# Eleven adding transfers of an attention kernel's MLP weights, issued in other rounds

## The chip, the cores and the metric

The kernel runs on one core of a Trainium2 chip. The metric is the time of one execution on the device in microseconds. Before the change it was 1013.88 us (median of 3 runs, 1013.76 to 1014.07).

The engines go by the names that the profile gives them: PE is TensorE (with PEld, its weight loads), DVE is VectorE, ACT is ScalarE, POOL is GpSimd, and SP issues transfers. Transfers run on 16 DMA engines that all queues share. Each engine runs its instructions in program order; semaphores hold an instruction back until what it reads is there.

## The reference

One layer of a diffusion backbone: a mixing sub-layer (pooling beside neighbourhood attention) and a squared-ReLU MLP, each inside an adaLN-modulated norm. 1024 latent tokens, 256 context tokens, width 1024, 8 heads of 64, all in fp32.

```python
h_x = _modulate(x, g_pre_mix[l], sh1, sc1)
h_c = _modulate(ctx, g_pre_mix[l], csh1, csc1)
u_x, q_x, k_x, v_x = _project(h_x, w_in[l])
u_c, q_c, k_c, v_c = _project(h_c, w_in[l])
attn_x = _neighbourhood_attention(q_x, k_x, v_x, k_c, v_c, rpb[l])
mix_x = jnp.concatenate([_pool_mixer(u_x, pool_w[l], pool_scale[l]), attn_x], axis=-1) @ w_out[l]
x = x + gt1 * _rmsnorm(mix_x, g_post_mix[l])
y_x = _sq_relu_mlp(_modulate(x, g_pre_mlp[l], sh2, sc2), w_mlp_in[l], w_mlp_out[l])
x = x + gt2 * _rmsnorm(y_x, g_post_mlp[l])

def _sq_relu_mlp(h, w1, w2):
    return jnp.square(jax.nn.relu(h @ w1)) @ w2
```

In the attention, each query sees an 8 x 16 window of the 16 x 64 grid with a position bias (`rpb`), and all 256 context keys, in one softmax.

## The kernel before, in words

Every product is split into a high and a low part (three matmuls for one, `three`), and the large products are made from seven block products with sums of blocks instead of eight. Two such sums of blocks of the MLP's second weight, `w2`, are this case's subject: t3q (8 groups) and t1d (8 groups), each group a 128 x 2 x 512 block of fp32, 512 KB, in DRAM. A group is made in two transfers. SP copies one block of `w2` there (`block_copied`, line 1327), and later GpSimd issues a transfer that reads another block of `w2` and adds it to what lies there (`block_summed`, which calls `add_to`, line 210). The list `block_sums` holds the sixteen adds in order, t3q's eight first; whoever calls `block_summed` takes the next. They are called sums below. The MLP reads t3q and t1d back hundreds of microseconds later.

Between the projections and the output projection lies the attention, 32 rounds (`for i in range(N)`), one for each pair of heads j and each block of 128 tokens m, in an order written out by hand. A round i issues, among others:

- `scores(i)`: TensorE, two heads' scores into two PSUM tiles;
- `biased(i, e)`: VectorE adds the bias table and takes the minimum; in the first of the two, `share(i - 1)` takes the reciprocals ri of unit i-1 and GpSimd spreads them over 64 columns into rb (line 1260). In the profile that is POOL L1260 COPY rb<-ri, rb9 for unit 9 and so on;
- in rounds 11, 19 and 27 two adding transfers of finished heads (`right_added`: y<-f and ss<-f), in rounds 15, 23 and 31 one more (f<-ss), all from GpSimd;
- `jobs`: a table of GpSimd's own work by round: the bias tables of the next heads (`built`, L1077), splits of operands into high and low parts (L1090, L1091: qP, kP, mix, wo), two small gathers (L816: sc2, s2);
- `block_copied`, then as many `block_summed` as the round's number stands in the table `SUMS`;
- `turn(i - 2)`: TensorE transposes, first rb of unit i-2, then its probabilities; a transpose's first step is a weight load (PEld L1276);
- `exps` (ScalarE), copies out of PSUM, and `values(i - 3)` (PE L1310).

GpSimd's instructions keep this order (`first_pool`, an ordering of that engine). So a sum stands on GpSimd behind the round's jobs and ahead of the next round's copy rb; and in GpSimd's DMA queue (q0) among the other adding transfers. The adding transfers of GpSimd take eight completion semaphores in turn.

After the rounds come the sums of the output projection. Loads of weights by SP (to_0w to to_3w, in `raw` and `page` buffers) are combined by adding transfers of GpSimd (to_0w<-in_w_out and to_1w<-in_w_out in round 31's wake, then y<-f, ss<-f, to_2w<-to_0w, to_3w<-to_1w). VectorE's products mp<-pox,Ga (line 1386, `out_kept`) write pages that to_0w and to_1w held, and so wait until the adds that read those have landed; TensorE's sums poz take the PSUM tile that these products read. Five more sums stand there, with rows 0 to 7 of the residual, and are not touched.

Of the kernel before, what the change touches and what calls it, by code (L numbers as in the profile page):

```python
# [103 lines left out]
def hybrid_block(ctx, tc, x, ctx_in, w_mod, mod_pages, w_u, b_mod, gp1, gp2, w_in, pool_w, rpb, w_out, w1, w2, vectors,  # L104
# [1081 lines left out]
    def block_summed():  # L1186
        to, of, g = block_sums.pop(0)
        add_to(to(g), of(g))
# [5 lines left out]
    with (  # L1194
# [132 lines left out]
        def block_copied():  # L1327
            to, i, g = block_copies.pop(0)
            nc.sync.dma_start(to(g), w2_block(i, 1, g))
# [2 lines left out]
        kks = (0, 1, 2, 3)  # L1332
        raw_o, wo = {}, {}
        LOADS = (16, 20, 26, 28)
        SUMS = (9, 11, 12, 14, 15, 16, 19, 22, 23, 27, 30)
        lows = []

        def high(src, hi, lo, pool=False):
# [73 lines left out]
        with in_order(ET.PE, ET.Activation, ET.DVE, ET.SP) as projected:  # L1412
# [34 lines left out]
            for i in range(N):  # L1447
# [26 lines left out]
                if block_copies and (i < 4 or 6 < i):  # L1474
                    block_copied()
                for _ in range(SUMS.count(i)):
                    block_summed()
# [1010 lines left out]
```

## Time and profile before

| | |
|---|---|
| median of 3 runs | 1013.88 us |
| the profiled execution | 1014.29 us, of which the span that the profile covers is 1012.5 us |
| PE busy | 1002.7 us, 99% of the span |
| DVE, ACT, POOL busy | 78%, 57%, 20% |
| granted TensorE clock | 0.999 |
| GpSimd's DMA queue (q0) | 18640 packets, 38.45 MB |
| SP's DMA queue (q1) | 111024 packets, 181.63 MB |
| attention's rounds | about 214 to 314 us |

Times in rows are microseconds from the start of the span. A row of the timeline has start, duration, engine, line, operation, output and inputs, and in brackets how long the engine stood idle before it and what ended that. A row of the waits has who waited for what, the total in us, how often, and the longest. A row of the DMA view has the median time from issue to landing.

### The profile page before, as it was taken

The numbers are of one execution on the slowest core, as the hardware profiler recorded it, in microseconds if no ns is written. First come the engines' busy times: TensorE is split into PE (matmuls) and PEld (weight loads), VectorE is DVE, ScalarE is ACT, GpSimd is POOL, SyncE is SP. The second block draws the span as 40 slices with busy tenths as digits, with TensorE's granted clock in tenths as the row PEclk, the third lists the DMA queues.
The fourth block names the chain that finished last, engine by engine and source line by source line (L and its number), as shares of the span: only waits on it lengthen the run. The fifth ranks groups of instructions, "written<-read, shape, count | busy, mean of one in ns | idle before, by whom it ended". The sixth has DMA issues, their size and how long they took to land.

```text
span 1012.5 us, 17059 instructions
## 1 busy us (share of the span) xinstructions
PE 1002.7 (99%) x6298; PEld 843.5 (83%) x6298; DVE 785.4 (78%) x1216; ACT 573.4 (57%) x988; POOL 203.7 (20%) x278
## 2 busy tenths in 40 slices
PE   8999999999999999999999999999999999999997
PEld 5788888878998888888888888888889888888886
DVE  5588767968885689879998888755797877877895
ACT  6672254448886746786555544555555455544451
POOL 4111200167985232410000000000001010021121
PEclk9999999999999999999999999999999999999999
DMA  9999799655989979986776667625999999579944
GB/s 365 392 295 323 248 260 310 210 154 198 229 183 247 233 196 273 298 210 202 262 250 219 204 201 235 210 75 188 357 354 302 289 339 310 161 212 315 305 180 163
DMA packets 146883, 252.13 MB, mean 249 GB/s; under 512 B 10416, under 2 KB 76848, under 8 KB 146800
## 3 DMA queue, kind: packets, MB, share of 16 engines
q1 hardware_dynamic: 111024, 181.63, 52.6%
q0 software_dynamic: 18640, 38.45, 19.7%
q10 hardware_dynamic: 17136, 30.97, 8.2%
q8 instruction: 49, 0.80, 0.3%
q14 instruction: 34, 0.28, 0.1%
HBM read 197.52 MB, written 69.22 MB: 263 GB/s over the span
## 4 chain that ended last, share of the span: by engine, by line
PE 97%; DVE 1%; ACT 1%; DMA 1%; POOL 0%; issue 0%; SPq 0%; DVEq 0%; POOLq 0%; ACTq 0%
PE pu L476 4%; PE pa L1310 3%; PE S L1223 3%; PE phx L221 3%; PE pyx L221 3%; PE phv L221 3%; PE phz L221 3%; PE pyx L222 3%; PE phx L222 3%; PE phx L223 3%; PE phv L223 3%; PE phz L223 3%; PE phz L222 3%; PE phv L222 3%; PE pyx L223 3%; PE pyz L221 1%
## 5 line engine op out<-in xcount | busy, mean ns | idle before, releaser
L1930 ACT ACTIVATE c<-c 128x512 f32<-128x512 f32 x48 | 30.3, 632 | 44.2 <-DVE c L2052 24.5
L1254 ACT ACTIVATE sp<-sp,nm 128x640 f32<-128x640 f32 (+1 forms) x64 | 51.4, 804 | 6.1 <-DVE ri L1258 4.8
L1243 DVE CUSTOM_DVE_ANT_0 sp<-S,tab 128x640 f32<-128x640 f32 (+1 forms) x56 | 44.5, 795 | 13.0 <-PE pz L1276 7.6
L169 ACT CAST wpS<-S 128x512 fp32r<-128x512 f32 x64 | 38.7, 616 | 28.0 <-PE phv L223 9.7
L221 PE MATMUL phx<-thB,wpA 128*128 128x512 f32 x128 | 50.2, 392 | 0.0
L222 PE MATMUL phx<-tlB,wpA 128*128 128x512 f32 x128 | 49.9, 389 | 0.0
L223 PE MATMUL phx<-thB,wpA 128*128 128x512 f32 x128 | 49.8, 389 | 0.0
L175 DVE TENSOR_TENSOR wpS<-S,wpS 128x512 fp32r<-128x512 f32 x64 | 43.4, 686 | 7.5 <-ACT wpS L169 7.4
L211 POOL DMA_DIRECT2D t<-in_w x16 | 19.3, 1208 | 105.5 <-DMA t<-t1d 61.9
L1931 ACT ACTIVATE c<-c 128x512 f32<-128x512 f32 x48 | 30.3, 630 | 15.1 <-DVE sa L2015 12.1
L238 POOL MEMSET accb<- 128x1024 f32 x1 | 1.0, 956 | 142.1 <-ACT c L1931 142.1
L221 PEld LDWEIGHTS phx<-thB,wpA 128*128 128x128 f32 x128 | 24.0, 188 | 5.5 <-ACT s L1983 0.4
L223 PEld LDWEIGHTS phx<-thB,wpA 128*128 128x128 f32 x128 | 24.0, 188 | 5.0
L222 PEld LDWEIGHTS phx<-tlB,wpA 128*128 128x128 f32 x128 | 24.0, 188 | 4.9
L1310 PE MATMUL pa<-pt,v 128*64 128x128 f32 x352 | 25.8, 279 | 0.0
L221 PE MATMUL phv<-thT,wpA 128*128 128x512 f32 x64 | 25.0, 391 | 0.0
L221 PE MATMUL phz<-thB,wpS 128*128 128x512 f32 x64 | 25.0, 391 | 0.0
L223 PE MATMUL phv<-thT,wpA 128*128 128x512 f32 x64 | 24.9, 389 | 0.0
L223 PE MATMUL phz<-thB,wpS 128*128 128x512 f32 x64 | 24.9, 389 | 0.0
L222 PE MATMUL phz<-tlB,wpS 128*128 128x512 f32 x64 | 24.9, 389 | 0.0
L221 PE MATMUL phy<-thT,wpS 128*128 128x512 f32 x64 | 24.9, 389 | 0.0
L222 PE MATMUL phy<-tlT,wpS 128*128 128x512 f32 x64 | 24.9, 389 | 0.0
(1200 smaller groups left out, 3683.0 us busy)
## 6 DMA issues: line engine op xcount, KB each, us to landing
hrA<-hdA SPq DMA_DIRECT2D x24, 512.0 KB, 7.5
wm<-in_mod_pages SPq DMA_DIRECT2D x16, 512.0 KB, 9.3
wa_0w<-in_w SPq DMA_DIRECT2D x16, 512.0 KB, 5.0
wa_1w<-in_w SPq DMA_DIRECT2D x16, 512.0 KB, 4.3
hdA<-c ACTq DMA_DIRECT2D x32, 256.0 KB, 2.2
hdS<-sa ACTq DMA_DIRECT2D x32, 256.0 KB, 2.6
hqS<-sb ACTq DMA_DIRECT2D x32, 256.0 KB, 4.1
b<-in_w SPq DMA_DIRECT2D x16, 512.0 KB, 8.6
```

What stands on the lines that cost most here:

```text
L169: nc.scalar.copy(hi, src)
L175: nc.vector.tensor_tensor(lo, src, hi.bitcast(F32), sub)
L221: nc.tensor.matmul(ps, ahi, bhi, start=first, stop=False, skip_group_check=more)
L222: nc.tensor.matmul(ps, ahi, blo, start=False, stop=False, skip_group_check=more)
L223: nc.tensor.matmul(ps, alo, bhi, start=False, stop=last, skip_group_check=more)
L476: nc.tensor.matmul(pus[b][j], wk(wgt, k, low, j * P, P), r, start=(k == 0 and n == 0), stop=(k == KT - 1 and n == 2))
L1223: nc.tensor.matmul(S[e][:, c0 : c0 + k[0].shape[1]], q[n_q][hs, cols], k[n_k][hs], start=(n_q + n_k == 0), stop=(n_q == 1))
L1243: nc.vector.tensor_tensor_reduce(out=to, in0=s, in1=bt, scale=1.0, scalar=BIG, op0=add, op1=ALU.min, accum_out=nm)
L1254: nc.scalar.activation(sp, sp, AF.Exp, bias=least[i, e], scale=-1.0, accum_out=sums[i][:, e : e + 1])
L1310: nc.tensor.matmul(pa[e * HD : (e + 1) * HD, cols], v[:, f : f + HD], turns[i][:, e, c] if c < 4 else fifths[i][:, :, (e + 1) * HD : (e + ...
L1930: nc.scalar.activation(r, src, AF.Relu)
L1931: nc.scalar.activation(r, r, AF.Square)
```

## The change

One table of round numbers is changed: the eleven sums of the rounds are issued in rounds 9, 10, 10, 12, 16, 18, 24, 25, 26, 29 and 30 in place of 9, 11, 12, 14, 15, 16, 19, 22, 23, 27 and 30. Their number, order and sizes stay.

```diff
@@ -1332,7 +1332,7 @@
         kks = (0, 1, 2, 3)
         raw_o, wo = {}, {}
         LOADS = (16, 20, 26, 28)
-        SUMS = (9, 11, 12, 14, 15, 16, 19, 22, 23, 27, 30)
+        SUMS = (9, 10, 10, 12, 16, 18, 24, 25, 26, 29, 30)
         lows = []
```

The order of instructions changes on GpSimd alone. GpSimd from round 10's copy (rb9) to round 12's (rb11), before and then changed; sc2 and tab00 are round 10's jobs, y0 and ss0 the adds of round 11, t3q0 a sum:

```order
L1260 COPY rb9_2867<-ri_9_2865 128x128
L816 DMA sc2_962<-gsc_2511 128x8x1
L1077 TENSOR_TENSOR tab00_2007<-msk_1900,U2_2803 128x128 x3
L1260 COPY rb10_2934<-ri_10_2932 128x128
L211 DMA y0_1345<-f0_2407 128x512
L211 DMA ss0_2107<-f0_2407 128x512
L211 DMA t3q0_2092<-in_w2 128x2x512
L1260 COPY rb11_3005<-ri_11_3003 128x128
```

```order
L1260 COPY rb9_2867<-ri_9_2865 128x128
L816 DMA sc2_962<-gsc_2511 128x8x1
L1077 TENSOR_TENSOR tab00_2007<-msk_1900,U2_2803 128x128 x3
L211 DMA t3q0_2092<-in_w2 128x2x512 x2
L1260 COPY rb10_2936<-ri_10_2934 128x128
L211 DMA y0_1345<-f0_2407 128x512
L211 DMA ss0_2107<-f0_2407 128x512
L1260 COPY rb11_3006<-ri_11_3004 128x128
```

Two sums now stand ahead of rb10, and ahead of y0 and ss0; the one behind ss0 is gone.

GpSimd in rounds 14 to 16, before and then changed; qP3 and mix0_5 are splits, f0<-ss0 is the add of round 15, which reads what ss0<-f0 of round 11 wrote:

```order
L1090 CAST qP3_0_3159<-q0_2_1970 128x512
L1091 TENSOR_TENSOR qP3_0_3159<-q0_2_1970,qP3_0_3159 128x512
L211 DMA t3q0_2092<-in_w2 128x2x512
L1260 COPY rb14_3227<-ri_14_3225 128x128
L211 DMA f0_2407<-ss0_2107 128x512
L211 DMA t3q1_2093<-in_w2 128x2x512
L1260 COPY rb15_3299<-ri_15_3297 128x128
L1090 CAST mix0_5_3304<-f1_2984 128x512
L1091 TENSOR_TENSOR mix0_5_3304<-f1_2984,mix0_5_3304 128x512
L211 DMA t3q1_2093<-in_w2 128x2x512
L1260 COPY rb16_3371<-ri_16_3369 128x128
```

```order
L1090 CAST qP3_0_3160<-q0_2_1970 128x512
L1091 TENSOR_TENSOR qP3_0_3160<-q0_2_1970,qP3_0_3160 128x512
L1260 COPY rb14_3227<-ri_14_3225 128x128
L211 DMA f0_2407<-ss0_2107 128x512
L1260 COPY rb15_3298<-ri_15_3296 128x128
L1090 CAST mix0_5_3303<-f1_2985 128x512
L1091 TENSOR_TENSOR mix0_5_3303<-f1_2985,mix0_5_3303 128x512
L211 DMA t3q1_2093<-in_w2 128x2x512
L1260 COPY rb16_3370<-ri_16_3368 128x128
```

The sums of rounds 14 and 15 are gone; round 16 keeps one.

GpSimd in rounds 24 to 26 and the start of 27, before and then changed; wo0_0 is a split of a weight, y2 the first add of round 27:

```order
L1260 COPY rb23_3868<-ri_23_3866 128x128
L1090 CAST mix0_6_3873<-f2_3558 128x512
L1091 TENSOR_TENSOR mix0_6_3873<-f2_3558,mix0_6_3873 128x512
L1260 COPY rb24_3939<-ri_24_3937 128x128
L1090 CAST qP3_1_3944<-q1_2_1902 128x512
L1091 TENSOR_TENSOR qP3_1_3944<-q1_2_1902,qP3_1_3944 128x512
L1260 COPY rb25_4008<-ri_25_4006 128x128
L1090 CAST wo0_0h_4013<-wor0_0_3277 128x512
L1091 TENSOR_TENSOR wo0_0l_4014<-wor0_0_3277,wo0_0h_4013 128x512
L1260 COPY rb26_4074<-ri_26_4072 128x128
L211 DMA y2_1441<-f2_3558 128x512
```

```order
L1091 TENSOR_TENSOR mix0_6_3870<-f2_3557,mix0_6_3870 128x512
L211 DMA t3q1_2093<-in_w2 128x2x512
L1260 COPY rb24_3937<-ri_24_3935 128x128
L1090 CAST qP3_1_3942<-q1_2_1902 128x512
L1091 TENSOR_TENSOR qP3_1_3942<-q1_2_1902,qP3_1_3942 128x512
L211 DMA t3q1_2093<-in_w2 128x2x512
L1260 COPY rb25_4007<-ri_25_4005 128x128
L1090 CAST wo0_0h_4012<-wor0_0_3276 128x512
L1091 TENSOR_TENSOR wo0_0l_4013<-wor0_0_3276,wo0_0h_4012 128x512
L211 DMA t1d_0_2084<-in_w2 128x2x512
L1260 COPY rb26_4074<-ri_26_4072 128x128
L211 DMA y2_1441<-f2_3557 128x512
```

Each of the three rounds now has a sum behind its split.

## The prediction

> **What bounds the kernel now.** I read the page's first and fourth parts first, then the stage of the change in stretches of three microseconds, then the waits inside it.
>
> ```profile
> PE 1002.7 (99%) x6298; PEld 843.5 (83%) x6298; DVE 785.4 (78%) x1216; ACT 573.4 (57%) x988; POOL 203.7 (20%) x278
> ...
> PE 97%; DVE 1%; ACT 1%; DMA 1%; POOL 0%; issue 0%; SPq 0%; DVEq 0%; POOLq 0%; ACTq 0%
> ```
>
> TensorE is busy for 99% of the span and makes 97% of the chain that ended last. So a transfer has no price of its own here: it costs what it makes TensorE wait, and there is next to nothing to win. GpSimd's 20% is an average over the program. In the attention stage, 214 to 322 us, it reads otherwise (columns: stretch, sum, then busy PE, PEld, DVE, ACT, POOL, the granted clock, the DMA share, GB/s):
>
> ```profile
> 254.00:257.00 3.00, 3.00 (x60) 2.76 (x56) 2.54 (x8) 2.79 (x8) 2.79 (x5) 1.00 1.01 156
> 296.00:299.00 3.00, 3.00 (x51) 2.73 (x51) 2.57 (x8) 2.56 (x8) 2.23 (x4) 1.00 1.12 223
> ```
>
> A round of attention is one such stretch, 2.8 to 3.0 us. GpSimd is nearly as full as TensorE, and the DMA engines are full too. TensorE depends on GpSimd once a round: rb(i), the copy at line 1260, is what turn(i) transposes first, and turn(i) runs in round i+2. The stage's waits name it:
>
> ```profile
> POOL rb L1260 <- DVE ri L1258: 11.8, 12, 2.3
> PEld pa L1276 <- POOL rb L1260: 0.3, 1, 0.3
> ```
>
> GpSimd often waits for its reciprocal, so it has time over in a dozen rounds; TensorE waited for the copy once by name. What counts is where the change uses up that time.
>
> **The change part by part.** Eleven sums leave rounds 9, 11, 12, 14, 15, 16, 19, 22, 23, 27, 30 and stand in 9, 10, 10, 12, 16, 18, 24, 25, 26, 29, 30. None is added, none grows. GpSimd's own rows (start, duration) around the first places:
>
> ```profile
> 248.77 1.22 POOL L211 DMA_DIRECT2D t3q<-in_w  x1 [0.19 <-issue]
> ...
> 252.71 1.28 POOL L1077 TENSOR_TENSOR tab<-msk,U 128x128 f32<-128x128 f32 x3
> 253.96 0.29 POOL L1260 COPY rb<-ri 128x128 f32<-128x128 f32 x1
> ...
> 255.08 1.18 POOL L211 DMA_DIRECT2D ss<-f  x1
> 255.64 1.81 POOL L211 DMA_DIRECT2D t3q<-in_w  x1
> ...
> 259.63 1.42 POOL L211 DMA_DIRECT2D t3q<-in_w  x1
> ...
> 264.64 1.29 POOL L1091 TENSOR_TENSOR qP<-q,qP 128x512 fp32r<-128x512 f32 x1
> 265.87 1.15 POOL L211 DMA_DIRECT2D t3q<-in_w  x1
> 266.61 0.70 POOL L1260 COPY rb<-ri 128x128 f32<-128x128 f32 x1
> 266.84 1.34 POOL L211 DMA_DIRECT2D f<-ss  x1
> 267.43 1.96 POOL L211 DMA_DIRECT2D t3q<-in_w  x1
> 268.47 1.22 POOL L1260 COPY rb<-ri 128x128 f32<-128x128 f32 x1
> ...
> 272.29 0.70 POOL L1260 COPY rb<-ri 128x128 f32<-128x128 f32 x1
> ...
> 314.08 1.28 POOL L211 DMA_DIRECT2D to_0w<-in_w_out  x1
> 315.41 1.22 POOL L211 DMA_DIRECT2D to_1w<-in_w_out  x1
> ```
>
> A sum is t3q<-in_w here, a copy rb<-ri. In round 14 the subtraction that starts at 264.64 ends at 265.93, and rb14 ends at 267.31: 1.38 us for a sum and a copy, and a copy alone is 0.29 (253.96), so a sum costs GpSimd 1.1 us. Two back to back have no row; nearest are the two large adds after the last round, 1.33 us apart (314.08 and 315.41). So two cost 2.2 to 2.66, and I take 2.4.
>
> *Round 10, two sums ahead of rb10.* The tables end where rb10 starts now, 253.96; with 2.4 and the copy's 0.29 it ends at 256.65. TensorE takes its copies by weight loads:
>
> ```profile
> 255.48 0.14 PEld L1276 LDWEIGHTS pa<-ident,rb 64*128 64x128 f32 x1
> 267.36 0.13 PEld L1276 LDWEIGHTS pa<-ident,rb 64*128 64x128 f32 x1
> 270.33 0.14 PEld L1276 LDWEIGHTS pa<-ident,rb 64*128 64x128 f32 x1
> ```
>
> The first is rb10's, at 255.48: late by 1.2 (1.0 to 1.45). Queued behind it on TensorE are the rest of turn(10), values(9) and the scores of round 13, so the whole stage moves. **+1.2.** The second is rb14's: the copy ended at 267.31 and the load came 0.05 later, so TensorE stood there; the only wait with that name is 0.3, and I take 0.2 (0 to 0.3). Round 14 loses its sum: **-0.2**. Rounds 11 and 12 carry the lateness on, y, ss and the s2 transfer standing in front as before, but TensorE has moved by 1.2 too and rb11 to rb13 just fit.
>
> *Round 15, the add f<-ss.* It reads ss, written by the add of round 11, and GpSimd stands still at it until that add has landed. The times from issue to landing, in the order of issue (sum of round 9, ss, sum of round 11, sum of round 12), and GpSimd's queue over 245 to 292 us:
>
> ```profile
> t3q<-in_w POOLq DMA_DIRECT2D x1, 512.0 KB, 11.6
> ss<-f POOLq DMA_DIRECT2D x1, 256.0 KB, 9.9
> t3q<-in_w POOLq DMA_DIRECT2D x1, 512.0 KB, 11.9
> t3q<-in_w POOLq DMA_DIRECT2D x1, 512.0 KB, 12.1
> ...
> q0 software_dynamic: 2780, 5.18, 63.9%
> ```
>
> With the starts above they land at 260.4, 265.0, 267.5 and 271.7: as they were issued. y stands between the first two and is as large as ss. 63.9% of 47 us is 30 us of all engines for 5.18 MB, 3.0 us for a 512 KB sum. Now ss is 1.8 us ahead of its reader. After the change two sums stand in front of y and ss that stood behind. The same five transfers then end with ss, at the latest when the five end now, 271.7; at the earliest at 260.4 + 2 x 3.0 + 2 x 1.5 = 269.4. I take 271.0, since the late end is measured with the same traffic on the other queue. The add then starts at 271.0; f and the copy take 1.28 (rb14's end to rb15's, 267.31 to 269.69, is 2.38 with a sum in it). rb15 ends at 272.28, for a load that would stand at 270.33 + 1.2 - 0.2 = 271.33. **+0.9** (0 to 1.6). Behind the waiting add stand rb15, the split of round 16 and its sum: that round takes 3.3 (rb15's end to rb16's, 269.69 to 272.99) where TensorE's takes 2.9. **+0.4** if the first is late.
>
> *Rounds 24, 25, 26: a sum each.* Their copies wait for the reciprocal now, and rb26 has its load at 302.30:
>
> ```profile
> 295.11 0.29 POOL L1260 COPY rb<-ri 128x128 f32<-128x128 f32 x1 [0.77 <-DVE ri L1258]
> ...
> 297.98 0.29 POOL L1260 COPY rb<-ri 128x128 f32<-128x128 f32 x1 [0.64 <-DVE ri L1258]
> ...
> 300.75 0.29 POOL L1260 COPY rb<-ri 128x128 f32<-128x128 f32 x1 [0.54 <-DVE ri L1258]
> ...
> 302.30 0.13 PEld L1276 LDWEIGHTS pa<-ident,rb 64*128 64x128 f32 x1
> ```
>
> The waits sum to 1.95; three sums take 3.3. The 1.35 that is left meets 1.26 from rb26's end, 301.04, to its load. **+0.1** (0 to 0.4). Rounds 22, 23, 27 gain only idle time.
>
> *After the stage.* Five sums now run from round 24 on, where two and the tail of two others did. The chain they reach (two adds of GpSimd, a product of VectorE, a matmul of TensorE, and both queues over 300 to 345 us):
>
> ```profile
> 336.24 0.86 POOL L211 DMA_DIRECT2D to_2w<-to_0w  x1 [9.46 <-DMA to_2w<-in_w_out]
> 337.47 0.86 POOL L211 DMA_DIRECT2D to_3w<-to_1w  x1 [0.37 <-issue]
> ...
> 344.45 0.69 DVE L1386 TENSOR_TENSOR mp<-pox,Ga 128x512 f32<-128x512 f32 x1 [1.77 <-DMA to_3w<-to_1w]
> ...
> 345.99 0.39 PE L221 MATMUL poz<-to_0h,S 128*128 128x512 f32 x1
> ...
> q0 software_dynamic: 2236, 4.73, 60.1%
> q1 hardware_dynamic: 3122, 6.26, 40.9%
> ```
>
> The matmul needs the bank that the product started at 344.45 frees, at 345.14: 0.85 us of room. That product waits for an add, the add for a load, and the load shares engines that the two queues fill to 101%. One sum more in that stretch is 3.0 us of engine time. If the DMA engines had room for it nothing moves; if the backlog of the rounds before comes on top (half a sum more) it is 4.5. I take the middle, 2.25, less 0.85: **+1.4** (0 to 3.6).
>
> The sums' own readers are far off, the first of them the loads of t1d from 750.4 us on (count, durations in ns, first and last start):
>
> ```profile
> L2139 SPq DMA_DIRECT2D t<-t1d x8: 325/658/3363, 750.4 to 835.1; - x8
> ```
>
> The order of the other four engines is the same as before.
>
> Sum: 1.2 - 0.2 + 0.9 + 0.4 + 0.1 + 1.4 = 3.8 us. The profiled execution took 1014.29 with a span of 1012.5, so it would show 1016.3 and 1018.1; it lies 0.4 above the median of the runs, 1013.88, to which I add: **1017.7 us**.
>
> [...]
>
> **The rivals.** *The queue has room.* If a 256 KB add does not wait for the sums in front of it, ss lands before 269.9 and f does not wait; if the spare 0.85 us at poz is not used up either, only round 10's own stall stays: 1.2 - 0.2 = +1.0, 1014.9, not to be told from before. It decides at those two points. For it: transfers on one queue run on sixteen engines side by side, and 101% is a mean that may hold gaps at the right place. Against it: the landings in order of issue, 60% of the engines in GpSimd's own queue. 25%.
>
> [...]
>
> *Nothing waits, and the old waits go.* rb could start 0.74 us after a sum's start (265.87, 266.61). If two sums cost only that, rb10 ends at 253.96 + 1.48 + 0.29 = 255.73, 0.25 late; round 14 gives back 0.2 to 0.3, and with no wait behind f or poz the time is 1013.9, at best 1013.6. For it: TensorE waits little anywhere. Against it: the copy after a sum lasted 0.70, not 0.29. 6%.
>
> *The backlog carries through.* All terms at their upper bounds: 1.45 - 0.2 + 1.6 + 0.4 + 0.4 + 3.6 = 7.25, 1021.1. For it: 101% on the engines. Against: several of them would have to be at the bound. 14%.
>
> **How the numbers follow.** Forecast 55%. Differences under 0.2%, 2.0 us, cannot be told from none here. Slower: forecast and backlog, 69%, and the edge of the queue rival 2%, 71%. Same: 26%. Faster by over 2 us: 3%, since the waits that the rows show gone sum to a few tenths. The range, 1014.2 to 1020.8, holds the forecast and the rival of the queue with room; it leaves out the rival without waits and the upper part of the backlog.
>
> **What would show it.** Right: the load of turn(10)'s copy waits about 1 us for GpSimd; f<-ss in round 15 waits for a DMA, 2 to 4 us; rb14 no longer holds TensorE; the to_3w add starts 1 to 3 us later relative to the last round and poz waits for the product. Wrong: a weight load of rb that never waits, or a stage of attention as long as before.

## The result, and the profile after

The changed kernel took 1024.69 us (median of 6 runs, 1019.28 to 1025.11), against 1013.88 us for the kernel before: a ratio of 1.0092, with a 95% interval of 1.0080 to 1.0103. It is slower, by 10.8 us where 3.8 were forecast. Two more sets of runs on other occasions gave 1021.46 and 1021.59 (ratios 1.0081 and 1.0074). The profiled execution shown here took 1022.3 us with a span of 1020.5.

The busy line, the clock by fortieths of the span and the chain, of the page of the changed kernel:

```profile
PE 1005.4 (99%) x6298; PEld 845.5 (83%) x6298; DVE 785.4 (77%) x1216; ACT 573.2 (56%) x988; POOL 203.4 (20%) x278
...
PEclk9999999999899999999999999999999999999999
...
PE 93%; DMA 2%; POOL 2%; issue 1%; ACT 1%; DVE 1%; SPq 0%; DVEq 0%; POOLq 0%; ACTq 0%
```

GpSimd's busy time is the same, 203.4 against 203.7. TensorE's grew by 2.7 us with the same 6298 matmuls, and one fortieth of the clock reads 8: some matmuls ran slower. The rest of the 8 us is idle time of TensorE. The waits of the attention stage say where:

```profile
POOL f L211 <- DMA ss<-f: 7.2, 1, 7.2
PEld pa L1276 <- POOL rb L1260: 5.6, 3, 4.2
...
PE pa L1276 <- POOL rb L1260: 4.9, 2, 4.0
```

GpSimd waits once for a transfer, for 7.2 us, where it did not wait before. TensorE's weight loads wait 5.6 us for GpSimd's copies, against 0.3 us before, and its matmuls wait 4.9 us in two places where none waited before. GpSimd's rows, in order of time, around the first two sums that stand together and around the wait:

```profile
253.91 2.37 POOL L211 DMA_DIRECT2D t3q<-in_w  x2
255.35 1.23 POOL L1260 COPY rb<-ri 128x128 f32<-128x128 f32 x1
255.59 1.87 POOL L211 DMA_DIRECT2D y<-f  x1
256.18 2.16 POOL L211 DMA_DIRECT2D ss<-f  x1
...
266.76 0.29 POOL L1260 COPY rb<-ri 128x128 f32<-128x128 f32 x1
274.26 0.91 POOL L211 DMA_DIRECT2D f<-ss  x1 [7.21 <-DMA ss<-f]
274.88 0.59 POOL L1260 COPY rb<-ri 128x128 f32<-128x128 f32 x1
```

And TensorE's first transposes of the two late copies, rb10 and rb15:

```profile
256.63 0.27 PE L1276 MATMUL pa<-ident,rb 64*128 64x64 f32 x1 [0.89 <-POOL rb L1260]
...
275.53 0.36 PE L1276 MATMUL pa<-ident,rb 64*128 64x64 f32 x1 [4.00 <-POOL rb L1260]
```

Stretches of two microseconds around the second (busy PE, PEld, DVE, ACT, POOL, then the granted clock, the DMA share, GB/s):

```profile
270.00:272.00 2.00, 1.53 (x22) 1.15 (x16) 1.29 (x5) 1.46 (x5) 0.00 (x0) 1.00 1.09 264
272.00:274.00 2.00, 0.00 (x0) 0.00 (x0) 1.21 (x5) 0.00 (x0) 0.00 (x0) 1.00 0.94 255
274.00:276.00 2.00, 0.47 (x8) 0.47 (x10) 0.00 (x0) 0.07 (x1) 1.74 (x3) 0.70 0.47 109
276.00:278.00 2.00, 2.00 (x27) 1.88 (x26) 0.69 (x1) 2.00 (x6) 1.91 (x3) 0.50 0.65 114
278.00:280.00 2.00, 2.00 (x18) 1.67 (x16) 0.29 (x1) 0.37 (x2) 1.92 (x4) 0.50 0.35 42
280.00:282.00 2.00, 2.00 (x32) 1.93 (x30) 0.98 (x4) 0.38 (x3) 0.71 (x1) 0.59 1.04 179
282.00:284.00 2.00, 2.00 (x36) 1.83 (x34) 1.46 (x5) 2.00 (x5) 1.86 (x3) 1.00 0.29 51
```

TensorE stands from 271.5 to 275.5. When it starts again the granted clock is 0.50, as it is from 274.8 to 281.6 (read in quarter microseconds). The twelve matmuls pa<-pt,v of that round take 1.55 us; such twelve take 0.88 in the kernel before, at a clock of 1.00.

The loss can be dated by the starts of the first rb transpose of each round: the distance from one to the next, less the same distance before the change. Three profiled executions of the changed kernel (the first above, two from the experiments), in us:

```
                                   first    second   third
round 10's late copy               +1.07    +1.05    +1.05
the wait for ss in round 15        +4.08    +2.42    +2.66
the round behind that wait         +2.38    +0.45    +1.50
other rounds                       +0.16    -0.09    -0.01
poz, after the stage               +0.28    +0.63    +2.08
near 398 us                        +0.24    +0.26    +0.18
sum                                +8.21    +4.72    +7.46
start of the stage                 -0.17    -0.28    -0.45
execution, against 1014.29 before  +8.0     +4.4     +7.0
```

The first line is steady. The wait, the round behind it and poz vary by 1.7 to 1.9 us each from execution to execution. The runs of the changed kernel spread over 6 us, while those of the kernel before lie within 0.5 us beside them and within 2.2 on every other occasion. No profiled execution is as slow as the median of the first six runs, 1024.69: the slowest shows 8.0 of the 10.8 us, and where the rest went is not shown.

### The profile page after: what moved, and what is told of

Same layout as the page of the kernel before. It is cut to its first block, busy times and chain, and to the rows that moved or that the text cites. A ratio compares the mean times of both kernels' runs of the same rounds, so it can differ in the third digit from the quotient of the medians.

```text
span 1020.5 us, 17064 instructions
## 1 busy us (share of the span) xinstructions
PE 1005.4 (99%) x6298; PEld 845.5 (83%) x6298; DVE 785.4 (77%) x1216; ACT 573.2 (56%) x988; POOL 203.4 (20%) x278
## 4 chain that ended last, share of the span: by engine, by line
PE 93%; DMA 2%; POOL 2%; issue 1%; ACT 1%; DVE 1%; SPq 0%; DVEq 0%; POOLq 0%; ACTq 0%
PE pu L476 4%; PE phx L221 3%; PE pyx L221 3%; PE phz L221 3%; PE phv L221 3%; PE pyx L222 3%; PE phx L222 3%; PE pyx L223 3%; PE phz L223 3%; PE phv L223 3%; PE phx L223 3%; PE phv L222 3%; PE phz L222 3%; PE pa L1310 3%; PE S L1223 2%; PE pyz L221 1%
## 5 line engine op out<-in xcount | busy, mean ns | idle before, releaser
L1295 DVE COPY pt<-T 128x512 f32<-128x512 f32 x31 | 21.3, 686 | 5.5 <-PE T L1276 5.5
L222 PE MATMUL phv<-tlT,wpA 128*128 128x512 f32 x64 | 24.9, 389 | 0.0
```

The costliest lines, as they stand in the source:

```text
L222: nc.tensor.matmul(ps, ahi, blo, start=False, stop=False, skip_group_check=more)
L1295: copy(turns[i].rearrange("p e i t -> p (e i) t")[:, :, h * HD : (h + 1) * HD], turned[i][h].rearrange("p (a t) -> p a t", a=8))
```

## The experiments

The theory after this reading: four prices, at round 10, at the wait for ss, at the clock behind it, and at poz. The rivals: that GpSimd or its queue is simply overfull, so that a wait taken out comes back elsewhere; that the clock fell for another reason; that the late sums matter more.

### The reader of ss, three rounds later

```diff
-                if 8 < i and i % 8 == 7:
-                    add_to(heads[i // 8 - 1][:, :512], sa2[i // 8 - 1])
+                if i in (18, 23, 31):
+                    k = {18: 0, 23: 1, 31: 2}[i]
+                    add_to(heads[k][:, :512], sa2[k])
```

> The changed kernel with one thing undone: the add f<-ss of head group 0 stands in round 18 instead of round 15, so that GpSimd does not meet it before ss has landed. Theory (the wait for ss in round 15 makes nearly all of the loss, and the TensorE gap it opens also halves the granted clock for some 6 us): no wait of 7 us on GpSimd, no gap of 4 us on TensorE, the clock stays at 1.00; what stays is round 10's own stall of 1.1 us less 0.2 in round 14: 1014.5 to 1015.3 us. Rival (GpSimd and its queue are simply overfull from round 10 on, and the wait only shows where it first surfaces): another copy is late instead, 1019 us or more. Rival (the sums of rounds 24 to 30 make part of the loss): 1016 to 1018.

Measured: 1017.02 us (1015.91 to 1017.63), ratio 1.0026 (1.0015 to 1.0036). GpSimd's rows of that kernel, f<-ss and, after the stage, its add for to_2w:

```profile
276.31 0.91 POOL L211 DMA_DIRECT2D f<-ss  x1 [0.25 <-issue]
...
339.72 0.86 POOL L211 DMA_DIRECT2D to_2w<-to_0w  x1 [11.37 <-DMA to_2w<-in_w_out]
```

VectorE's product that the poz matmul waits for, in the same kernel:

```profile
348.08 0.69 DVE L1386 TENSOR_TENSOR mp<-pox,Ga 128x512 f32<-128x512 f32 x1 [1.82 <-DMA to_3w<-to_1w]
```

TensorE's row of that matmul. The bracket names the VectorE operation next to the product; the product itself ends at 348.77:

```profile
348.91 0.47 PE L221 MATMUL poz<-to_0h,S 128*128 128x512 f32 x1 [1.19 <-DVE a L1721]
```

The wait, the gap and the low clock are gone, and with them 5.2 of the 8.2 us of the first profiled execution (8.21 to 3.05). But ss landed as late as ever, at 274.1, so its lateness is no consequence of the wait. 3.05 us stay, where 0.5 to 1.3 were expected: 1.06 in round 10, 0.40 in round 18, where the moved add now stands ahead of a copy, and 1.47 at poz. The rival on the late sums is right for that last part.

### The early and the late part of the change alone

```diff
-        SUMS = (9, 10, 10, 12, 16, 18, 24, 25, 26, 29, 30)
+        SUMS = (9, 10, 10, 14, 15, 16, 19, 22, 23, 27, 30)    # early only
+        SUMS = (9, 11, 12, 14, 16, 18, 24, 25, 26, 29, 30)    # late only
```

> Only the first three entries of the change: sums in rounds 9, 10, 10, 14, 15, 16, 19, 22, 23, 27, 30. Theory (the two sums that now stand ahead of y and ss): the whole loss is there, 1021 to 1026 us, with the wait of f<-ss in round 15 and the halved clock behind it. Rival (the late sums of rounds 24 to 30 or the sum in round 12): at most round 10's own stall, 1015 to 1016.

> The change without its first part: sums in rounds 9, 11, 12, 14, 16, 18, 24, 25, 26, 29, 30, so the rounds up to 14 are as before and the rest as in the change. Theory: f<-ss does not wait, rounds 24 to 26 hide their sums, poz loses a few tenths: 1013.6 to 1014.6 us. Rival (late sums collide with the loads after the stage, the prediction's +1.4, or more): 1015 to 1018.

Measured: early only 1020.76 us (1020.70 to 1022.82), ratio 1.0071 (1.0056 to 1.0086); late only 1015.24 (1014.65 to 1016.01), ratio 1.0012 (1.0003 to 1.0021). GpSimd's add f<-ss with the early part alone:

```profile
272.85 0.91 POOL L211 DMA_DIRECT2D f<-ss  x1 [5.77 <-DMA ss<-f]
```

TensorE's transpose of rb15 behind it:

```profile
275.30 0.27 PE L1276 MATMUL pa<-ident,rb 64*128 64x64 f32 x1 [4.28 <-POOL rb L1260]
```

The early part makes as long a stall and a low clock behind it, for 3.4 us, and loses nothing at poz; its median is 0.2 us under what was expected. The late part leaves the 32 rounds as long as before (91.88 us from the first rb transpose to the last, against 91.95) and loses 0.67 at poz and 0.21 near 398 us. Its median is 0.6 us over the top of what was expected, so here the rival is right.

### GpSimd made late without a transfer

The kernel before, with copies of GpSimd of its own, 16 and 7 of them:

```diff
+                if i == 15:
+                    spare = att.tile([P, P], F32, tag="spare", name="spare")
+                    for _ in range(16):        # and 7
+                        nc.gpsimd.tensor_copy(spare, shares[14])
```

> The kernel before, with 16 copies of 128x128 of GpSimd alone (0.29 us each, 4.6 us) set behind f<-ss in round 15; no transfer is added or moved. rb15 ended 0.64 us ahead of its load, so TensorE stands for about 4.0 us, as it did in the changed kernel. Theory (an idle TensorE of that length is itself what halves the clock): about 0.50 granted for some 6 us afterwards, and 1020 to 1021.5 us, 6.4 or more over before. Rival (the clock fell in the changed kernel for another reason, such as the transfers): the clock stays near 1.00 and the time is 1017.9 to 1018.5, the stall alone.

> The kernel before, with 7 copies of GpSimd behind f<-ss in round 15. 16 of them took 6.4 us and held TensorE for 5.3, so 7 take 2.8 and hold it for 1.7. Theory (the clock falls only after a long gap): 0.4 more in the round behind at most, the clock stays at 1.00: 1015.5 to 1016.2 us. Rival (any stall of this stage costs clock too): 1017 us or more.

> The kernel with 7 copies of GpSimd in round 15 once more. In its first profiled execution TensorE stood for 1.75 us and the clock was 0.50 for the 3.4 us from 272.0 on. Theory (the clock is set by how much of a fixed stretch of about 3.4 us was idle, and the stretches do not begin with the stall): the same stall of 1.7 to 1.9 us, with a clock that falls in some executions and not in others, so that the runs lie in two groups, 1015.5 to 1016.5 and 1017.3 to 1018.5. Rival (a stall of 1.75 us always costs the clock): all runs within 0.5 us of 1017.5.

Measured: 16 copies, 1021.85 us (1021.33 to 1021.89), ratio 1.0075 (1.0060 to 1.0090). 7 copies, 1017.48 (1016.31 to 1020.46), ratio 1.0037 (1.0023 to 1.0051), and once more 1017.45 (1016.20 to 1017.70), ratio 1.0032. GpSimd's row of the 16 copies:

```profile
267.32 6.42 POOL L1475 COPY spare<-rb 128x128 f32<-128x128 f32 x16
```

TensorE's transpose of rb15 behind them:

```profile
275.76 0.36 PE L1276 MATMUL pa<-ident,rb 64*128 64x64 f32 x1 [5.29 <-POOL rb L1260]
```

And the stretch that follows, with a granted clock of 0.50:

```profile
276.00:278.00 2.00, 2.00 (x28) 1.88 (x28) 0.69 (x1) 1.84 (x6) 1.91 (x3) 0.50 0.96 125
```

With 7 copies, TensorE's transpose of rb15:

```profile
271.69 0.27 PE L1276 MATMUL pa<-ident,rb 64*128 64x64 f32 x1 [1.75 <-POOL rb L1260]
```

And the stretch that follows it, again at 0.50:

```profile
272.00:275.25 3.25, 3.25 (x38) 2.80 (x36) 0.78 (x2) 2.43 (x7) 3.16 (x5) 0.50 1.12 218
```

No transfer was added or moved, and the clock falls all the same: the idle time does it. Of the 7.0 us with 16 copies, 5.4 are the stall (the copies took 0.40 each with what lies between, not 0.29, so it was longer than meant) and 1.4 the round behind it. The second theory failed: a stall of only 1.75 us also cost the clock, in both profiled executions with 7 copies, and 1.3 to 1.6 us more than the stall. Read in quarter microseconds, the low clock lasts 3.4 us with the early part alone (275.83 to 279.25), with 16 copies (275.26 to 278.67) and with 7 (272.0 to 275.41), and 6.8 us, twice that, in the first execution of the changed kernel. It does not begin where the stall ends: 0.3 us behind it in one execution with 7 copies, 1.4 us behind it in the other. The third expectation, two groups of runs, came true as far as the times go: 1016.20 and 1016.50, and 1017.45, 1017.60 and 1017.70. But both profiled executions are of slow ones, so how the fast ones escaped was not seen in a trace.

### The changed kernel twice more, and with the gap filled

> The changed kernel once more, unchanged, for a second profiled execution: the first took 1022.3 us where the median is 1024.7. Theory: round 10's 1.1 us as before; what differs is when the last engine lands ss, and so the gap on TensorE and the length of the halved clock, or the 0.3 us at poz, which was up to 1.5 in the kernel with the later f<-ss. Rival: a difference outside 250 to 355 us.

> The changed kernel beside the one with the filled gap: round 10's 1.06 us again, ss landed at 272 to 275, TensorE standing for 2.3 to 4.5 us in round 15's wait, and 1021 to 1025 us.

The third experiment of this group sets transposes of an older copy into the place that rb15's overwrite:

```diff
+            for _ in range(56 if i == 15 else 0):
+                both(lambda h: sides[h][:, :HD], lambda hs: shares[i - 1][hs])
             both(lambda h: sides[h][:, :HD], lambda hs: shares[i][hs])
```

> The changed kernel with 56 pairs of transposes of rb14 ahead of those of rb15, into the place that rb15's overwrite: TensorE has about 3.1 us of work of no use where it stood for 2.3 to 4.0 us. Theory (a TensorE that does not stand keeps its clock): the granted clock stays at 1.00 behind the wait, which itself stays (the 3.1 us of filling and what of the wait is longer): 1018.5 to 1020 us, and in the same runs the changed kernel is 1.5 to 4 us slower. Rival (the idle time is not what lowers the clock): 0.50 for 3.4 us or more all the same, and the time of the changed kernel or longer.

Measured: the changed kernel 1021.46 us (1018.71 to 1023.44) and 1021.59 (1018.72 to 1023.51); with the gap filled 1022.08 (1021.68 to 1023.48), ratio 1.0084 (1.0067 to 1.0101). TensorE's transpose of rb15 in the second execution of the changed kernel:

```profile
273.81 0.27 PE L1276 MATMUL pa<-ident,rb 64*128 64x64 f32 x1 [2.33 <-POOL rb L1260]
```

Two stretches of that execution, with the clock at 1.00:

```profile
272.00:274.00 2.00, 0.19 (x6) 0.20 (x8) 1.15 (x5) 0.00 (x0) 1.46 (x3) 1.00 0.85 231
274.00:276.00 2.00, 2.00 (x40) 1.76 (x40) 0.75 (x2) 1.88 (x6) 1.92 (x3) 1.00 0.96 206
```

Here ss landed at 272.3 and TensorE stood for 2.33 us, longer than the 1.75 above, and the clock did not fall: the round behind lost 0.45, not 1.3 to 2.4. So the length of the stall alone does not decide. With the gap filled the clock is 1.00 in every stretch, of which three:

```profile
272.00:274.00 2.00, 2.00 (x68) 2.00 (x66) 1.64 (x5) 0.18 (x2) 1.32 (x3) 1.00 1.07 268
274.00:276.00 2.00, 2.00 (x72) 2.00 (x68) 0.00 (x0) 0.13 (x2) 1.91 (x3) 1.00 1.05 257
276.00:278.00 2.00, 1.68 (x31) 1.29 (x27) 0.69 (x1) 2.00 (x6) 1.92 (x4) 1.00 0.76 91
```

That is what the theory said of the clock. The time missed its 1018.5 to 1020: the filling lasted longer than the wait that was left (ss landed at 272.4), and poz took 1.78. Keeping the clock by useless work won nothing.

### One sum ahead instead of two, and both stalls out

```diff
-        SUMS = (9, 10, 10, 12, 16, 18, 24, 25, 26, 29, 30)
+        SUMS = (9, 10, 11, 12, 16, 18, 24, 25, 26, 29, 30)    # one ahead
+        SUMS = (9, 10, 11, 12, 16, 18, 19, 22, 23, 27, 30)    # both out, with f<-ss in round 18 as above
```

> The change with one sum less ahead of y and ss: sums in rounds 9, 10, 11, 12, 16, 18, 24, 25, 26, 29, 30. Round 10's stall is gone, since one sum alone ends rb10 in time or up to 0.2 us late; the late sums keep their price, which was 0.7 to 1.5 us at poz where they stood alone. Theory (each sum ahead puts ss off by about half of the 9 us that two put it off, from 265.0 to 274.0): ss lands near 269.5, f<-ss waits 2 to 4 us, TensorE under 1 us, the clock stays: 1014.6 to 1016.2 us. Rival (what makes ss late is its slowest engine, with a lag of 5 us whatever stands ahead): ss lands near 271 to 272, TensorE stands for 1 to 2 us more: 1016.5 to 1018.

> All three prices taken out: sums in rounds 9, 10, 11, 12, 16, 18, 19, 22, 23, 27, 30 (never two in a row, and the late ones as in the kernel before), and f<-ss of head group 0 in round 18. Theory (round 10, the wait for ss, and the late sums carry the whole loss): 1013.4 to 1014.2 us, like the kernel before or a few tenths under it, since rb14 no longer holds TensorE. Rival (the sums of rounds 12 and 18, or the later f<-ss, cost something of their own): 1014.8 us or more.

Measured: one ahead 1016.86 us (1016.18 to 1018.30), ratio 1.0027 (1.0017 to 1.0038); both out 1015.59 (1015.29 to 1016.01), ratio 1.0015 (1.0006 to 1.0025). With one ahead ss landed at 269.5, as the theory said, and f<-ss no longer holds TensorE; poz took 1.18. The time is 0.7 us over what the theory gave, and lies where the rival had it, for another reason: rounds 11 to 13 lost 0.7 us, in both kernels. GpSimd there, with both out:

```profile
259.44 2.37 POOL L211 DMA_DIRECT2D t3q<-in_w  x1
260.19 1.92 POOL L1260 COPY rb<-ri 128x128 f32<-128x128 f32 x1
```

The weight load of the copy that follows, in the same kernel:

```profile
262.16 0.14 PEld L1276 LDWEIGHTS pa<-ident,rb 64*128 64x128 f32 x1 [0.57 <-POOL rb L1260]
```

No two sums stand together here, and yet a copy is late: GpSimd has next to no gap from the end of round 9 to round 14 (the rows of before run on from 251.74 to 268), so what is added there shows as a late copy two rounds on. f<-ss in round 18 cost another 0.8 there and behind it. The theory that three places carry the whole loss fell, and the rival is right: with their prices taken out, these two took their place.

### SyncE's copies out of the way

```diff
-                if block_copies and (i < 4 or 6 < i):
+                if block_copies and (i < 4 or 15 < i):
```

> The changed kernel with SyncE's eight 512 KB copies of t1d in rounds 16 to 23 instead of 7 to 14, so that the other queue leaves the engines to GpSimd's adds up to round 15. Theory (ss is late by the sums ahead of it in its own queue): ss lands as in the changed kernel, last engine near 274, and the time stays at 1020 to 1026 us. Rival (the slowest engine is held up by the other queue's copies): the last engine lands ss within 2 us of the median, at 266 to 270, f<-ss waits 0 to 3 us, the clock stays at 1.00, and the time is 1014.5 to 1017.

Measured: 1017.11 us (1016.15 to 1018.58), ratio 1.0029 (1.0019 to 1.0039). GpSimd's f<-ss of the first two head groups:

```profile
267.06 0.91 POOL L211 DMA_DIRECT2D f<-ss  x1 [0.17 <-issue]
...
292.42 0.86 POOL L211 DMA_DIRECT2D f<-ss  x1 [2.22 <-DMA ss<-f]
```

The rival is right. The landings of the first ss, as the trace has them by DMA engine (first, ninth and last of sixteen):

```
before             262.0   263.8   265.0
changed            267.7   269.0   274.0
changed, second    267.5   269.8   272.3
changed, third     267.3   270.0   272.2
one ahead          265.9   266.9   269.5
copies late        265.0   265.5   266.3
```

With the same sums ahead of it, ss lands 6 to 8 us earlier and its engines finish within 1.3 us of one another once the other queue's copies are gone. f<-ss of round 15 does not wait. The copies now meet the second head group's adds in rounds 19 to 23, and there, where nothing waited before, f<-ss waits 2.22 us. The profiled execution is 2.3 us over before: 1.07 in round 10, 0.8 where GpSimd works without a gap behind that wait and its copies come late, and 0.57 at poz. The median is 3.2 over.

So the first ss lands earlier once SyncE's copies are away: at 266.3, where it was 272.2 to 274.0. But the copies also ran beside the adds before the change, when the last engine was 1.2 us behind the ninth (265.0 and 263.8). Why it falls back by 2.2 to 5.0 us behind more sums is not shown by any run.

### A second sum where GpSimd waits

The kernel before, with only round 14's sum moved, to round 9:

```diff
-        SUMS = (9, 11, 12, 14, 15, 16, 19, 22, 23, 27, 30)
+        SUMS = (9, 9, 11, 12, 15, 16, 19, 22, 23, 27, 30)
```

> The kernel before with only the sum of round 14 moved, to a second one in round 9: sums in rounds 9, 9, 11, 12, 15, 16, 19, 22, 23, 27, 30. Theory (GpSimd works without a gap from round 10 to round 14, so a sum there is paid in full, but in round 9 it waits 1.2 us for its reciprocal, which covers the second sum): no stall at rb9 or rb10, where two sums in round 10 cost 1.06; rb14's wait goes; ss lands near 269.5, as with one more sum ahead, and f<-ss waits up to 3 us without holding TensorE by more than 0.5: 1013.6 to 1014.8 us. Rival (two sums in a row cost TensorE about 1 us wherever they stand): 1015 us or more.

Measured: 1016.00 us (1014.25 to 1020.11), ratio 1.0025 (1.0015 to 1.0034). GpSimd's rows, in round 9 and at f<-ss:

```profile
248.54 2.40 POOL L211 DMA_DIRECT2D t3q<-in_w  x2 [0.20 <-issue]
250.93 0.31 POOL L1260 COPY rb<-ri 128x128 f32<-128x128 f32 x1
...
268.90 0.91 POOL L211 DMA_DIRECT2D f<-ss  x1 [3.00 <-DMA ss<-f]
```

TensorE's transpose of rb15:

```profile
271.35 0.27 PE L1276 MATMUL pa<-ident,rb 64*128 64x64 f32 x1 [1.15 <-POOL rb L1260]
```

Two sums in a row cost TensorE nothing here (2.78 and 2.89 us between the rounds, 2.79 and 2.87 before): the second fills the 1.2 us in which GpSimd waited for its reciprocal. So it is not two in a row that costs, it is GpSimd's lack of a gap. The time still missed what the theory gave: ss landed at 268.6, its reader waited 3.00, and with that round's own sum behind the add TensorE stood for 1.15.

None of these kernels is faster than the one before, and no run points to one that would be by more than the 0.2 us of rb14's wait.

## Why the prediction was right or wrong

The median lies beyond the range's upper end, 1020.8; the direction and the places were right. The largest loss came from the term that the prediction had third in size, and the clock had no term.

- *TensorE bounds, and a transfer costs what it makes TensorE wait.* Right. Every loss found is idle time of TensorE or its slower clock.
- *Round 10, +1.2 (1.0 to 1.45).* Right: 1.05 to 1.07 in three executions. Two sums took GpSimd 2.37 us where 2.4 was taken.
- *Round 14, -0.2.* About half of it: 2.84 us instead of 2.92 between those rounds, and the wait with that name is gone.
- *Round 15, +0.9 (0 to 1.6).* **This is the step that failed, by size.** The add waits for ss in that round and rb15 is late behind it, as said; but the add waited 7.2 us in the first execution where 2 to 4 were named, and TensorE lost 4.08, 2.42 and 2.66 us. The wrong number is the landing of ss, 271.0 with 271.7 as its latest: it was 274.0, 272.3 and 272.2. The bound was the landing of the last of the five transfers before the change, and held only if the slowest engine fell back no further than then: there the ninth engine landed at 269.9 and the last at 271.7. Now the ninth engine was in time (269.0 to 270.0 against the forecast 271.0); but the reader starts when the last engine has landed, and that one lagged by 2.2 to 5.0 us. With SyncE's copies moved it lagged 0.8 and ss landed at 266.3. So the same traffic on the other queue, on which the prediction rested its late end, did not make that end an upper bound.
- *Round 16, +0.4.* Right where the clock held: 0.45 in the second execution.
- *No term for the clock.* The round behind the stall took 1.50 and 2.38 where the clock fell. That follows from the first miss: 0.9 us of idle time would have been too short by any row here (the shortest with a fall behind it is 1.75), and 1.15 in the last experiment's profiled execution left the clock at 1.00.
- *Rounds 24 to 26, +0.1.* Right: nothing measurable.
- *poz, +1.4 (0 to 3.6).* Right in mechanism and within its bounds: 0.28, 0.63 and 2.08. It goes with the late sums: 0.57 to 1.78 in the five other kernels that have them, nothing in the six executions whose late sums stand as before. The room was overrated: 0.85 us was taken, and in the eight executions with the late sums poz loses what the to_2w add is late by, less 0.40 to 0.49. That the middle of a range from 0 to 3.6 came near the three is in part luck: the add was late by 0.75, 1.13 and 2.58.

The row for the worst of them, the to_2w add in the third execution of the changed kernel, where it waited 9.46 before:

```profile
343.57 0.86 POOL L211 DMA_DIRECT2D to_2w<-to_0w  x1 [12.04 <-DMA to_2w<-in_w_out]
```

It starts 20.72 us after the last rb transpose; before it was 18.14. 2.58 less 0.45 is 2.13, and 2.08 was lost.

The rivals: the queue had no room, so the first is wrong, and so is the one without waits. The backlog came through, though not as it was put: not all terms at their bounds but one of them beyond it, with the clock on top. It was given 14% and 1021.1 us, which is about where the later runs lie.

## What to carry to other kernels

When an engine that issues transfers also feeds the bottleneck, look for the stretch in which it has no gap: there one more sum of 1.2 us cost the bottleneck 0.7 us, and two in one round 1.1, while a single wait of 1.2 us elsewhere covers a whole sum. For a transfer that something waits on, ask when its last engine lands and what the other queues do then, not when the mean would be done: up to 5 us lay between the ninth engine and the last here. And a stall of TensorE needs a second term for the clock behind it: behind stalls of 1.75 us and longer it was 0 to 2.4 us in these traces.

## What the runs showed of the hardware

- TensorE's granted clock fell to 0.50 in or after idle times of 1.75 (twice), 2.57, 4.0, 4.28 and 5.29 us, and not after 2.33 and 1.15, nor after the 1.80 us at poz in the third execution of the changed kernel, where the matmul behind the stall took 0.47 us, as it did behind 1.19 us in the kernel with the later reader of ss:

```profile
352.70 0.47 PE L221 MATMUL poz<-to_0h,S 128*128 128x512 f32 x1 [1.80 <-DVE ns L1722]
```

- The length of a stall alone does not decide: 2.33 us passed and 1.75 did not. The low clock lasted 3.41 or 3.42 us in five executions and 6.83 in the first of the changed kernel. The clock in the profiled execution before the change and in that one (the first record of 1.00, then each change, in us from the start of the span):

```
           first 1.00, then changes           from one to the next
before     6.03, 1009.54                      1003.52
changed    5.15, 274.80, 281.63, 1018.91      269.65, 6.83, 737.28
```

- These distances are 294, 79, 2 and 216 times 3.413 us. In the six executions where the clock fell in round 15's stall or behind it, TensorE was idle for this long in the 3.41 us just ahead of the fall (7 copies twice, the changed kernel's third, its first, the early part alone, 16 copies; us):

```
clock falls at                         272.00   273.36   273.56   274.80   275.83   275.26
idle in the 3.41 us just ahead of it     1.75     1.75     2.40     3.27     2.89     3.41
```

- An estimate: counted on from 273.56 in steps of 3.413 us, a step of the changed kernel's third execution ends at 352.07, and the 1.80 us at poz (350.90 to 352.70) lie in two of them, with 1.17 and 0.63 us, each less than 1.75. How the 2.33 us lie to such steps is not shown, nor at what idle time between 1.17 and 1.75 us the clock would fall.
- The 256 KB add ss<-f took 9.9 us from issue to landing before, with one sum and y queued ahead of it. With three sums and y ahead it took 17.8 us beside the copies of the other queue, and 10.3 us with these moved. The changed kernel's row of transfer issues between 250 and 280 us:

```profile
ss<-f POOLq DMA_DIRECT2D x1, 256.0 KB, 17.8
```

- A small loss near 398 us, 0.2 us, goes with the late sums. No run was made for it, and its cause is open.
- Rounds 5 to 7, ahead of every moved sum, differ by up to 0.5 us between executions of different kernels. Terms of a few tenths in a single execution are no finding.
